# A hybrid decoder layer on one core: FFN buffers with a place of their own, and the last projection rows, norms and additions issued in other places

## The chip, the cores and the metric

The kernel runs on one core of a Trainium2 chip. The metric is the device time of one execution in microseconds (us). A core has a matrix engine (TensorE, PE in the profile, with its weight loads as PEld), a vector engine (VectorE, DVE), a scalar engine (ScalarE, ACT), a general engine (GpSimd, POOL) and a queue that issues transfers (SyncE, SP). Matrix products are written to PSUM, which has eight banks of 128 x 512 floats; everything else lies in SBUF, 128 partitions wide.

## The reference

One inference step of a one-layer decoder with D = 1024, for 16 meta rows, a prompt of 2048 rows and 8 x 4 sample rows. The rows that come out are 2048 + 32.

```
hp = layer_norm(concat(meta, x_prompt)); hs = layer_norm(x_sample)
mixed = token_mixers(h)            # one input projection, 4 retention heads, 4 gated DeltaNet heads,
                                   # gates, then  concat(o_r, o_g) @ w_out   (1024 x 1024)
h = layer_norm(ALPHA * h + mixed, ln1_g, ln1_b)
gu = h @ w_gate_up                 # 1024 x (2 * 2816)
f = (silu(gu[..., :2816]) * gu[..., 2816:]) @ w_down
y = layer_norm(ALPHA * h + f, ln2_g, ln2_b)
```

The states of both head groups and the last rows of the convolution are outputs too. All is float32. The change concerns only what stands after the token mixers: the output projection with its norm (ln1), the SwiGLU FFN, and its norm (ln2).

## The kernel before

Each float32 product is made of three fp32r products: both operands are split into a high part and a rest, and `mm3` (line 368) issues high x high, high x low and low x high into one PSUM accumulator. `split` makes the high part with a cast (line 311, on ScalarE) and the rest with a subtraction (line 318, on VectorE or GpSimd). The program is written with a framework that places buffers, orders the instructions of each engine by a simulated readiness with the program's order as priority, and adds all waits. A pool is a region of SBUF or PSUM; a tag with `bufs=n` has n slots. Pools are stacked: a pool that is opened after another one is closed takes its place, and then waits for the last use of what lay there. SP issues every transfer, in the order the framework gave it.

The kernel has three stages. `attention` (to about 1300 us) makes the mixed heads and stores them in device memory (`mixd`). `project` goes over 17 row tiles (16 of 128 rows, one of 32 sample rows) in the order of `BLOCKS`:

- `load(i)`: the mixed values into a staging tile `mr` (own tag, two slots), the residual rows into `oy`, and the split into `mh` and `ml`.
- `project(i)`: two halves of 512 columns, 24 matmuls each, in PSUM tag `d` (three banks, pool p_d); line 1199 adds the residual; `layer_norm` (ScalarE line 302, VectorE line 304 for the gain, GpSimd line 306 for the bias); the rows go to `yd`.
- `transposed(i)`: eight 128 x 128 transposes (line 1209) into PSUM tag `tr` (three banks, pool p_t), copies to `xr`. When both tiles of a pair are there, `sums` makes four differences on GpSimd (line 1222) and stores seven parts into `bd`: these are the seven token operands of a Strassen-Winograd scheme.

Its loop runs `project(i)`, the load of the next tile, and `transposed(i - 2)`; the last two iterations only transpose. The weights of the projection are four pieces, each loaded in two halves through the tag `raw` (two slots) and split into `wh`, `wl`.

`ffn` goes over three blocks of three row pairs. Block 0 has the prompt tiles P0 to P3 and the sample rows (n = 272 columns: two pairs of 128 and one of 16), blocks 1 and 2 six prompt tiles each (n = 384). `tokens(bi)` loads the seven token operands through the tag `fr` (four slots) and splits them into one tile each (pool f_b, ScalarE and VectorE). Then, for each of the 22 feature tiles f:

- `weights(f)` loads 1 MB of gate and up weights through `fr`, makes four sums and differences `S` on GpSimd (line 1288) and splits them; it is a generator that `step` advances.
- `gateup` issues seven products of 12 matmuls, into the PSUM tags X (two banks), Y, Z and W (pool p_g), with additions between them (line 1325), and applies the gate (lines 1331 to 1333). The result is `fh`, `fl`, in two halves: half 0 holds the first row tile of each pair, half 1 the second.
- `down` multiplies two feature tiles at a time with w_down (`dh`, `dl`): for every row tile and half of columns it issues 6 matmuls (3 for the last two feature tiles, which go one by one) into a `d` bank and adds the result to the row buffer `y` (line 1380). It is a generator too; `step`, called after each product of a later feature tile, takes one piece of it. In the last feature tile of all it takes three pieces.
- With the last pair of feature tiles of a block, each row tile's norm follows its additions: `layer_norm` with two statistics (line 286), their combination (line 289), eleven steps on one column (lines 263 to 270 and 299), then lines 302, 304 and 306. In the very last row tile lines 293 and 295 take the place of these three. The rows are then stored (line 1383).

The row buffers `y` are loaded (line 1429) after feature tile 1 of each block. The FFN's pools are opened after the projection's pools and its weights are closed, so they lie over them.

## Time and profile before

| | |
|---|---|
| median of 3 runs | 3042.78 us (3040.59 to 3043.56) |
| the profiled execution | 3041.72 us, span of its instructions 3039.9 us |
| granted TensorE clock, mean | 0.977 |
| TensorE busy | 2865.1 us (94%) |
| VectorE busy | 2184.7 us (72%) |
| ScalarE busy | 1148.7 us (38%) |
| GpSimd busy | 1039.0 us (34%) |
| memory traffic | 384.75 MB, mean 127 GB/s |

A line of a timeline has the start and the duration in us, the engine, the line of the kernel, the operation, and what it writes and reads. A line of the chain of work has start, duration, engine, tile and line; "issue" is time in which an engine waited for nothing that the profile shows. A line of a stage table has the stage, its length, and for PE, PEld, DVE, ACT and POOL the busy time with the number of instructions, then the granted clock, the share of the transfer engines and GB/s. A line of a tile's view has the operation, the number of records, the least, median and greatest duration in ns, the first and last start, and the shapes.

### The profile page before, as it was taken

To read this page: it belongs to the slowest core of one execution; us is meant where nothing else is said; L and a number is where in the kernel's file an instruction comes from. 1 tells how busy PE (TensorE), PEld (TensorE's weight loads), DVE (VectorE), ACT (ScalarE), POOL (GpSimd) and SP (SyncE) were. 2 spreads that over 40 slices of the span, in tenths; PEclk is the share of its full clock that TensorE was granted. 3 is DMA by queue.
4 is the path that set the end of the run, shared out by engine and by line. 5 is a ranking of instruction groups with operands and counts; after the bars stand their busy time and mean duration, and the time that the engine had idled before them with its cause. 6 is when DMAs were issued, how large, how long until landed. Compare 5 with 4: busy or idle time off the path is not lost.

```text
span 3039.9 us, 47059 instructions
## 1 busy us (share of the span) xinstructions
PE 2865.1 (94%) x17930; PEld 2550.1 (84%) x17930; DVE 2184.7 (72%) x4547; ACT 1148.7 (38%) x2571; POOL 1039.0 (34%) x927
## 2 busy tenths in 40 slices
PE   7999999999999999999869999899999989999995
PEld 6888888888888887978758889789999988999994
DVE  7777677766776676667677777886666688666667
ACT  2434444444444435432243333433333343233331
POOL 1222222221222131236545444453343335343332
PEclk9999999999999999999979999999999999999998
DMA  7544544443444333366542222431212244121211
GB/s 272 200 172 161 182 147 156 157 151 147 156 152 153 122 114 122 111 206 205 191 167 84 91 84 97 149 124 59 77 59 74 76 136 139 56 77 62 71 63 42
DMA packets 132274, 384.75 MB, mean 127 GB/s; under 512 B 18144, under 2 KB 53520, under 8 KB 115664
## 3 DMA queue, kind: packets, MB, share of 16 engines
q1 hardware_dynamic: 132048, 381.74, 36.0%
q8 instruction: 141, 2.31, 0.3%
q14 instruction: 85, 0.70, 0.1%
HBM read 294.14 MB, written 87.56 MB: 126 GB/s over the span
## 4 chain that ended last, share of the span: by engine, by line
PE 59%; DVE 21%; issue 6%; POOL 6%; ACT 4%; DMA 3%; SPq 0%; POOLq 0%; ACTq 0%; DVEq 0%
PE pj L368 18%; PE d L368 16%; PE Y L368 4%; PE X L368 4%; POOL S L1288 4%; PE Z L368 4%; PE W L368 3%; DVE dl L318 2%; DVE s34l L318 1%; ACT s34h L311 1%; DMA fr<-bd 1%; DVE cacc L822 1%; ACT junk L773 1%; DVE y L1380 1%; DVE lnst L286 1%
## 5 line engine op out<-in xcount | busy, mean ns | idle before, releaser
L368 PE MATMUL pj<-wh,xT 128*128 128x256 f32 (+2 forms) x2176 | 458.2, 294 | 8.4 <-ACT wh L311 4.2
L368 PE MATMUL pj<-xT,wh 128*128 128x512 f32 (+1 forms) x1280 | 379.8, 381 | 1.8 <-ACT cpre L806 1.1
L368 PEld LDWEIGHTS pj<-wh,xT 128*128 128x128 f32 (+1 forms) x2176 | 352.5, 187 | 13.1 <-ACT wh L311 4.4
L368 PE MATMUL pj<-wl,xT 128*128 128x256 f32 (+3 forms) x1088 | 309.8, 285 | 0.5 <-POOL wl L318 0.5
L368 PE MATMUL d<-dl,fh 128*128 128x512 f32 (+1 forms) x748 | 299.9, 401 | 9.2 <-DVE dl L318 8.6
L368 PE MATMUL d<-dh,fh 128*128 128x512 f32 (+1 forms) x748 | 294.0, 394 | 8.1 <-DVE y L1380 8.0
L368 PE MATMUL d<-dh,fl 128*128 128x512 f32 (+1 forms) x748 | 297.6, 398 | 2.1 <-POOL fl L318 2.1
L318 POOL TENSOR_TENSOR fl<-ta,fh 128x384 fp32r<-128x384 f32 (+1 forms) x66 | 70.9, 1074 | 642.7 <-ACT fh L311 642.7
L1288 POOL TENSOR_TENSOR S<-fr 128x512 f32<-128x512 f32 x132 | 209.8, 1607 | 168.9 <-DVE s34l L318 108.3
L1380 DVE TENSOR_TENSOR y<-y,d 128x512 f32<-128x512 f32 (+1 forms) x352 | 238.8, 680 | 31.4 <-PE d L368 31.2
L368 PEld LDWEIGHTS pj<-xT,wh 128*128 128x128 f32 x1280 | 211.9, 194 | 25.2 <-issue 3.4
L368 PE MATMUL pj<-xT,wl 128*128 128x512 f32 (+1 forms) x640 | 229.6, 359 | 0.0
L368 PEld LDWEIGHTS pj<-wl,xT 128*128 128x128 f32 (+1 forms) x1088 | 204.5, 188 | 0.9 <-POOL wl L318 0.8
L368 PEld LDWEIGHTS d<-dl,fh 128*128 128x128 f32 (+1 forms) x748 | 138.0, 184 | 40.3 <-DVE dl L318 22.3
L368 PEld LDWEIGHTS d<-dh,fl 128*128 128x128 f32 (+1 forms) x748 | 138.1, 185 | 35.5 <-POOL fl L318 2.6
L318 DVE TENSOR_TENSOR a11l<-fr,a11h 128x512 fp32r<-128x512 f32 x66 | 52.3, 792 | 158.1 <-ACT a11h L311 158.1
L368 PEld LDWEIGHTS d<-dh,fh 128*128 128x128 f32 (+1 forms) x748 | 137.9, 185 | 30.7 <-DVE y L1380 11.3
L311 ACT CAST a11h<-fr 128x512 fp32r<-128x512 f32 x66 | 41.0, 621 | 291.9 <-DMA fr<-gu 291.9
L368 PE MATMUL X<-b,a11h 128*128 128x384 f32 (+1 forms) x528 | 125.5, 322 | 18.1 <-ACT b L311 13.9
L822 DVE SCALAR_TENSOR_TENSOR cacc<-cpre,cw,cacc 128x512 f32<-128x512 f32 (+1 forms) x144 | 115.8, 805 | 32.0 <-ACT cacc L820 30.5
L368 PE MATMUL Y<-t,s34h 128*128 128x384 f32 (+1 forms) x528 | 128.8, 328 | 8.5 <-DVE u L1325 4.3
L368 PEld LDWEIGHTS pj<-xT,wl 128*128 128x128 f32 x640 | 122.7, 192 | 16.8 <-issue 0.8
(333 smaller groups left out, 7809.5 us busy)
## 6 DMA issues: line engine op xcount, KB each, us to landing
fr<-gu SPq DMA_DIRECT2D x132, 512.0 KB, 3.9
wh<-parts SPq DMA_DIRECT2D x45, 1024.0 KB, 5.0
wl<-parts SPq DMA_DIRECT2D x45, 1024.0 KB, 6.7
fr<-dn SPq DMA_DIRECT2D x66, 512.0 KB, 3.9
parts<-wh SPq DMA_DIRECT2D x15, 1024.0 KB, 5.3
parts<-wl SPq DMA_DIRECT2D x15, 1024.0 KB, 6.9
raw<-wret SPq DMA_DIRECT2D x16, 512.0 KB, 5.2
raw<-wgd SPq DMA_DIRECT2D x16, 512.0 KB, 7.1
```

The costliest lines, as they stand in the source:

```text
L286: i = nc.vector.bn_stats(out=st[:, o], in_=x)
L311: i = nc.scalar.copy(out=h, in_=src)
L318: i = (nc.vector if el == "dve" else nc.gpsimd).tensor_tensor(out=l, in0=src, in1=h.bitcast(F32), op=ALU.subtract)
L368: self.nc.tensor.matmul(out, lhsT=a(k), rhs=b(k), start=first and k == 0 and i == 0, stop=last and k == kn - 1 and i == 2, skip_group_chec ...
L773: nc.scalar.activation(out=junk, in_=p[:, j, :], func=AF.Square, accum_out=sq[:, a, t:t + 1])
L822: nc.vector.scalar_tensor_tensor(out=ac, in0=pre[:, i:i + N], scalar=w(i), in1=ac, op0=ALU.mult, op1=ALU.add)
L1288: op = lambda o, x, z, f: nc.gpsimd.tensor_tensor(out=o, in0=x, in1=z, op=f)
L1380: nc.vector.tensor_tensor(out=ys, in0=ys, in1=p, op=ALU.add)
```

## The change

- The order of the blocks: block 0 is now P0 to P5, block 1 P6 to P11, block 2 P12 to P15 and the sample rows (n = 272). The projection follows this order, so the sample rows come last.
- The FFN's pools f_r (loads), f_a (split weights), f_s (sums), f_b1 (the first two token operands, b11 and t2) and f_y (row buffers) are opened at the other end of SBUF, before the projection, and no longer over its buffers. So are the two PSUM pools. The projection's accumulators and its transposes both use the three `d` banks. `mr` is gone: the mixed values are staged in `raw`, which the output weights use too. `xr`, the differences `T` and the last two projected rows lie in the row buffers of f_y.
- The transposes of the last two projected tiles become a generator, `rest`, whose pieces are issued between the products of the FFN's first feature tile.
- The norms between blocks: `layer_norms` takes all row tiles of a group (the first tiles of the pairs, or the others) and makes the small steps once, on up to three columns. It is a generator as well and is issued piece by piece (`chores`) between later products. Each row tile's store is followed by the load of the next block's row buffer.
- The second piece of each token operand is subtracted on GpSimd, in blocks 1 and 2.
- The last feature tile of all: the products are in another order (`late`), the additions of the first row tiles come before the last product, and the split is on VectorE. `finish` then makes the other three row tiles: six accumulators in six banks, to each of which the row buffer is added by a matmul with the identity, in float32. `layer_norms` reads the sums from PSUM.

```diff
-    Block([(_P(0), _P(1), 128), (_P(2), _P(3), 128), (0, NS // 2, NS // 2)]),
-    Block([(_P(i), _P(i + 1), 128) for i in (4, 6, 8)]),
-    Block([(_P(i), _P(i + 1), 128) for i in (10, 12, 14)]),
+    Block([(_P(i), _P(i + 1), 128) for i in (0, 2, 4)]),
+    Block([(_P(i), _P(i + 1), 128) for i in (6, 8, 10)]),
+    Block([(_P(12), _P(13), 128), (_P(14), _P(15), 128), (0, NS // 2, NS // 2)]),
...
+    def layer_norms(self, work, g, b, pool, sums=None):
...
+        for i, (x, rows) in enumerate(work):
+            st = pool.tile([128, 2, 6], F32, tag="lnst", name="lnst")[:rows]
+            for o in range(2):
+                nc.vector.bn_stats(out=st[:, o], in_=sums[i][o] if sums else x[:, 512 * o:512 * o + 512])
+            nc.vector.bn_aggr(out=mv[:rows, i], in_=st)
+            yield
+        r = self.rsqrt(mv[:, :, 1], T, 128, pool, 1.0, LN_EPS)
...
+            if sums and i == T - 1:
...
+            for o, p in zip(at, src) if sums else [(slice(0, D), x)]:
+                nc.scalar.activation(out=x[:, o], in_=p, func=AF.Identity, scale=r[:rows, i:i + 1], bias=nm[:rows, i:i + 1])
+            nc.vector.tensor_tensor(out=x, in0=x, in1=g[:rows], op=ALU.mult)
+            for u, o in enumerate(at):
+                (nc.vector if sums and u else nc.gpsimd).tensor_tensor(out=x[:, o], in0=x[:, o], in1=b[:rows, o], op=ALU.add)
...
+        spare = lambda i: self.fy.tile([128, D], F32, tag=f"y{i}", name="spare")
...
-                raw = op.tile([128, 8, 128], F32, tag="mr", name="mr")[:, :, :rows]
+                raw = self.raw.tile([128, 4, 256], F32, tag="raw", name="raw").rearrange("p a b -> p (a b)").rearrange("p (a b) -> p a b", a=8)[:, :, :rows]
...
-            for i in range(N + 2):
-                if i < N:
-                    project(i)
-                    if i and i + 1 < N:
-                        load(i + 1)
+            for i in range(N):
+                project(i)
+                if i and i + 1 < N:
+                    load(i + 1)
                 if i >= 2:
-                    transposed(i - 2)
+                    for _ in transposed(i - 2):
+                        pass
+        return rest()
...
+                    product(Z, "s1", "t1")
+                    add(z5, u3, Z)
+                    add(u2, u2, Z)
+                    step(5)
+                    late(fh, fl)
+                    X = ps("X")
+                    product(X, "s4", "b22")
+                    add(u2, u2, X)
+                    swish(u2, z5, 1, "tb")
...
+            def finish(bi, fs, w, fi):
...
+                banks = [(pd, "d")] * 3 + [(pg, t) for t in "YWZ"]
...
+                        down1(blk, fs, w, fi, i, n, p, False)
+                        nc.tensor.matmul(p, lhsT=self.ident[:rows, :rows], rhs=y[i][:rows, 512 * n:512 * n + 512], start=False, stop=True)
...
-                        self.split(r, h[:, o:o + m], l[:, o:o + m], "act", "dve")
+                        self.split(r, h[:, o:o + m], l[:, o:o + m], "act", "pool" if u and bi else "dve")
...
-            units = []
+            units, chores = [rest], []
...
-                        if (bi, f) == end:
-                            per = 3
-                        else:
-                            per = 1 if f % 2 or i >= 2 else 0
-                        for _ in range(per):
-                            while units and next(units[0], self) is self:
-                                units.pop(0)
+                        for _ in range(3 if (bi, f) == end else 1 if f % 2 or i >= 2 or (bi, f) == (0, 0) else 0):
+                            some(units)
+                        for _ in range(2 if f == 2 else 1):
+                            some(chores)
                         next(ws, None)
...
-            with self.weights_es:
-                self.attention()
-                self.project()
-            self.ffn()
+            with ExitStack() as late:
+                with self.weights_es:
+                    self.attention()
+                    self.fr = self.pool("f_r", bufs=4, es=late, side="right")
+                    self.fa = self.pool("f_a", es=late, side="right")
+                    self.fs = self.pool("f_s", es=late, side="right")
+                    self.fb = self.pool("f_b1", es=late, side="right")
+                    self.fy = self.pool("f_y", es=late, side="right")
+                    self.pg = self.pool("p_g", space=PSUM, es=late)
+                    self.pd = self.pool("p_d", bufs=3, space=PSUM, es=late)
+                    rest = self.project()
+                self.ffn(rest)
```

231 lines of the change are left out of this document (150 added, 81 removed).

## The prediction

> **What bounds the kernel now.** I read the page first (busy shares, then the 40 slices), then one table of stages, then inside each bad stage the chain of work and the timeline. The page first:
>
> ```profile
> span 3039.9 us, 47059 instructions
> PE 2865.1 (94%) x17930; PEld 2550.1 (84%) x17930; DVE 2184.7 (72%) x4547; ACT 1148.7 (38%) x2571; POOL 1039.0 (34%) x927
> ...
> PE   7999999999999999999869999899999989999995
> ```
>
> TensorE is busy 94% of the span, so nothing that keeps the products as they are can gain more than some 175 us. The dips in the slices are the start, slice 19-20, slices 25 and 32, and the last one. The stage table (us, then busy time of PE, PEld, DVE, ACT, POOL, granted clock, DMA share, GB/s) puts sizes to them:
>
> ```profile
> 1290.00:1325.00 35.00, 30.68 (x172) 24.88 (x171) 20.87 (x55) 15.82 (x35) 7.12 (x3) 1.00 0.76 242
> 1325.00:1505.00 180.00, 180.00 (x851) 145.95 (x850) 128.77 (x259) 47.15 (x58) 103.62 (x74) 1.00 0.62 195
> 1505.00:1590.00 85.00, 47.99 (x279) 42.36 (x278) 61.23 (x75) 34.44 (x59) 44.94 (x32) 0.76 0.50 174
> 1930.00:2010.00 80.00, 65.21 (x320) 56.91 (x319) 78.22 (x139) 36.91 (x55) 38.60 (x27) 0.96 0.51 168
> 2460.00:2545.00 85.00, 72.58 (x332) 64.58 (x331) 83.51 (x157) 34.49 (x50) 41.95 (x27) 0.90 0.45 154
> 2996.00:3039.90 43.90, 11.37 (x40) 6.72 (x38) 37.59 (x108) 7.24 (x7) 13.86 (x11) 0.68 0.18 72
> 1540.00:1550.00 10.00, 9.11 (x50) 8.39 (x51) 6.49 (x12) 5.56 (x11) 0.00 (x0) 0.79 0.69 208
> ```
>
> TensorE idles 37.0 us at the passage from the output projection to the FFN (85 - 47.99), 14.8 and 12.4 us at the two passages between FFN blocks, 32.5 us in the tail, and 4.3 us where the projection starts. Inside the projection it never idles. Busy time at a lower clock is lost too: 9.11 us at 0.79 is 1.9 us, and the first passage has more of it before 1540. I count that passage as 41 us, the block passages as 16 each (their clocks 0.96 and 0.90), 110 us in all with the tail and the start. The change touches every one of these places and, outside them, only the projection.
>
> **First passage (project to ffn), term +30.** The chain of work there, in order of time:
>
> ```profile
> 1494.86 10.94 PE d L368 x48
> ...
> 1515.54 1.27 POOL oy L306
> ...
> 1523.79 2.03 DMA bd<-T
> 1525.88 4.07 DMA fr<-gu
> ...
> 1534.93 1.60 POOL S L1288
> ...
> 1540.07 1.50 PE X L368 x5
> ```
>
> The last projection matmul ends at 1505.8 (1494.86 + 10.94); then follow the last norm (to 1516.8), the last transposes and differences, their stores, and only then (1525.88) the first weight load, because the FFN buffers lie over the projection's. The change gives f_r, f_a, f_s, the first two token tiles and f_y their own place, so that the loads, casts and S sums of feature tile 0 and the tiles b11 and t2 need nothing of the projection's end (block 0 becomes P0 to P5, whose parts are stored in the first half of the projection). The last two tiles' transposes are issued between the first products instead. What is late next are the other five token tiles: f_b lies over the projection's weights, so their casts can start only when its last matmul is done.
>
> ```profile
> L311 ACT CAST b<-fr x5: 617/622/1055, 1926.8 to 1951.7; 128x512 fp32r<-128x512 f32 x3, 128x1024 fp32r<-128x1024 f32 x2
> L318 DVE TENSOR_TENSOR b<-fr,b x5: 686/693/1218, 1927.5 to 1953.1; 128x512 fp32r<-128x512 f32 x3, 128x1024 fp32r<-128x1024 f32 x2
> fr<-bd SPq DMA_DIRECT2D x14, 512.0 KB, 3.6
> ```
>
> A 1536-column tile costs ACT 1.05 + 0.62 = 1.7 us, VectorE 1.22 + 0.69 = 1.9 us, and 768 KB of load. Four fr buffers can hold t1 and b21 before the end, so from the last projection matmul t1 is ready at about +3.2 and b21 at +5.5; t3, t4 and b22 wait for a free buffer, 3.6 us of landing and 1.9 us of VectorE, which I put at +9.5, +12.5 and +15.5. A product at n = 384 is 12 matmuls of 384 columns: with 48 matmuls of 512 in 10.94 us, 0.228 each, an estimate of 0.17 each, 2.0 us. Seven take 14 us, the transposes 1.8, so feature tile 0 ends near +17.5, 2 us late. Feature tile 1's weights queue behind the tokens on SP (land near +16.5), then two S sums of 1.60 and a split: about 4 us late. The last norm's VectorE work, earlier in the program, competes: 5 us. That leaves 11 of 41. Ends: 5 left (+36) if the last is hidden; 21 left (+20) if none of the loads really moves ahead of the projection's end.
>
> **Block passages, +10 and +6.** VectorE is 98% busy in both (78.22 of 80, 83.51 of 85), so it is the bound. What fills it:
>
> ```profile
> 1930.00:2010.00 80.00, 9.44 (x15) 0.96 0.51 168
> 1930.00:2010.00 80.00, 10.95 (x15) 0.96 0.51 168
> 1930.00:2010.00 80.00, 2.60 (x5) 0.96 0.51 168
> 1930.00:2010.00 80.00, 0.70 (x5) 0.96 0.51 168
> ```
>
> These are lines L269, L270, L299 and L264: the one-column steps of five layer norms. With four kinds of 0.14 us (L263 to L267) a norm's 11 small steps cost 1.89 + 2.19 + 0.52 + 0.56 = 5.2 us, 0.47 us each. layer_norms does up to three rows' statistics at once: 13 steps for a group, two groups, 26 steps instead of 55, so 13.6 us less. The second piece of each token tile goes to POOL: 7 x 0.69 = 4.8 us less on VectorE. That is 18 us less than 78, below the 65 us of products, so VectorE stops being the bound. Next late are the token loads (four buffers, tiles replaced one by one as the last feature tile frees them) and the gate weights behind them on SP. The rows also go through SP in a new order, each y load right behind its out store; a wait there holds the next gu load queued behind it. I leave 6 us of 16 at the first and 10 at the second passage, where the last block has 272 columns (1.5 us a product) over the same queue. Ends for both together: +5 and +26.
>
> The split moved to POOL has its own price. The trace has the same one-column step beside a POOL operation and without one (start, duration, engine):
>
> ```profile
> 1461.96 2.52 POOL L1222 TENSOR_TENSOR T<-xr 128x512 f32<-128x512 f32 x2
> 1462.05 1.21 DVE L270 SCALAR_TENSOR_TENSOR rqy<-rqt,rqy 128x1 f32<-128x1 f32 x1
> ...
> 1467.14 0.16 DVE L270 SCALAR_TENSOR_TENSOR rqy<-rqt,rqy 128x1 f32<-128x1 f32 x1
> ```
>
> So a VectorE step can stretch to the POOL operation's 1.2 us. The splits above have medians of 0.69 in a stage where POOL is half busy, so I take no extra charge. The Trainium skill ("SBUF — State Buffer", the term "shared port pair") says that VectorE and GpSimd arbitrate for one port pair, held for a whole instruction, and that the loser fully blocks; the 1.21 against 0.16 agrees. By that rule seven POOL splits of 1.2 us could stop VectorE for 8 us a block, more than the 4.8 saved, and the sum below would be about 38 instead of 42.
>
> **Tail, +7.** Now the tail is VectorE's: TensorE waits for the additions, and the norms run one by one.
>
> ```profile
> PE d L368 <- DVE y L1380: 6.5, 4, 3.0
> 2996.14 0.56 DVE L1325 TENSOR_TENSOR u<-u,Z 128x384 f32<-128x384 f32 x1 [1.24 <-PE Z L368]
> 2999.68 1.01 POOL L318 TENSOR_TENSOR fl<-tb,fh 128x384 fp32r<-128x384 f32 x1 [4.95 <-ACT fh L311]
> 3012.91 0.63 PE L368 MATMUL d<-dl,fh 128*128 128x512 f32 x1
> 3033.43 2.92 POOL L306 TENSOR_TENSOR y<-y,b 128x512 f32<-128x512 f32 x2 [3.11 <-DVE y L304]
> L674 PE MATMUL pj<-ub,rkd x16: 587/587/692, 71.3 to 363.6; 32*128 32x512 f32 x16
> ```
>
> After it, from the end A of the last gate/up product: sum, tanh and split take 4.55 us now (2996.14 to 3000.69); with 272 columns about 3.5, and 1 more for the first group's norm on VectorE. Then six groups, each three matmuls of 0.228 and the identity addition. That one is full fp32: the nearest row has 16 records for 8 such matmuls of 512 columns at 587 ns, against about 390 for fp32r that start every 228, so about 2 x 0.42 = 0.85. Six times 1.53 is 9.2. TensorE idled 4.5 us before; the matmul at 3012.91 takes 0.63 instead of 0.39 after a wait of 3.0, so the first of them run slow: +2. Then the last statistics and 13 small steps without POOL, 3.5; two rows of (1.21 + 0.67) and four half-row steps of 0.74, 6.7; store and end as now, 3039.9 less the last POOL addition's end at 3036.35, 3.5. Together 29.4, of which 4.1 is work that must run anyway: 25.3 lost against 32.5. Ends: 2 (the small steps stretch) and 15 (the first group's norm hidden, no slow clock).
>
> **What the change costs, -7 and -4.** The staging tile mr shares the raw ring (two buffers) with the four output weights. The rows of now:
>
> ```profile
> 1286.67 1.58 SPq L340 DMA_DIRECT2D raw<-wout  x2
> 1296.62 1.00 SPq L1183 DMA_DIRECT2D mr<-mixd  x2
> 1301.46 1.04 ACT L311 CAST mh<-mr 128x1024 fp32r<-128x1024 f32 x1
> 1302.59 4.73 POOL L318 TENSOR_TENSOR ml<-mr,mh 128x1024 fp32r<-128x1024 f32 x2 [17.02 <-ACT mh L311]
> 1316.16 24.44 PE d L368 x107
> ```
>
> Today weights and two rows of mixed values load side by side. Afterwards mr of tile 0 holds one raw buffer until its subtraction ends near 1305, half of the second weight comes after that, and mr of tile 1 comes last of ten loads. At 4.5 us a load and 2 us a split I get tile 1 ready at 1325.5 and two tiles done by 1336.4 (48 matmuls later); now the 107 matmuls that end at 1340.6 close the third tile, so two are done at 1329.7: -6.7, taken as -7, ends -2 (the order is better than I trace it) and -11.
>
> The projection's transposes now share the three "d" banks. An accumulator must be evacuated while the eight transposes run:
>
> ```profile
> 1470.41 0.87 PE tr L1209 x8
> 1469.96 0.68 DVE L1199 SCALAR_TENSOR_TENSOR oy<-oy,d 128x512 f32<-128x512 f32 x1
> 1471.28 0.67 DVE L1199 SCALAR_TENSOR_TENSOR oy<-oy,d 128x512 f32<-128x512 f32 x1
> ```
>
> Here it would be free at 1471.95, 0.67 after the transposes; at prompt tiles it is free in time. Fifteen tiles at 0 to 0.9 us (the transposes' own 0.87 at most, by this row): I take -4, ends 0 and -13. Weights and two token tiles add some 8 us to VectorE's 128.77 of 180, hidden there. Splitting feature half 1 on VectorE and the reordering of the blocks cost nothing elsewhere: the product count is the same.
>
> **Sum.** 30 + 10 + 6 + 7 - 7 - 4 = 42 us. The profiled execution took 3041.72 us, 1.06 below the median of 3042.78, so the forecast is 3001. All ends together give 3 to 75 us.
>
> **Rivals.** (1) The loads do not really run ahead: the scheduler keeps them behind the projection on SP's queue or behind late buffers. Then the first passage gains 20, the blocks 8, the tail 4, and the costs stay at 11: 21 us, 3022. For it: the order on SP decides, and it is not visible. Against: wout and mr loads did run ahead of the attention's end. (2) All passages close: VectorE relieved, tokens ahead: 36 + 24 + 12 - 5 = 67, 2976. Against it are the token loads with four buffers. (3) Slower: the projection, the one stage at 180.00 of 180, stalls at every tile because three banks wait for VectorE, which is 72% busy and now has splits of 1.2 us in its queue. The gains without that term are 46, so from 2.7 us at each of 17 tiles it decides; at 4 us it costs 68 and the kernel takes about 3064. Against it: the wait seen is 0.7. (4) No change, gains eaten by the start and the banks: 3042.
>
> **How the numbers follow.** Forecast 57% (its own range 2985 to 3012), rival 1 20%, rival 2 12%, rival 3 7%, no change 4%. The range 2974 to 3027 leaves out part of rivals 1 and 2, and all of rival 3 and of no change. Differences under 0.2% (6 us) this measurement can't tell from none. Forecast, rivals 1 and 2 are faster, together 0.89; same 0.04; slower 0.07.
>
> **What would show it.** Right: first weight and b11 loads long before the projection's last matmul; TensorE idle under 15 us in the first passage, clock near 1; VectorE below 90% at the block passages with 26 small steps; the tail from the last gate/up product near 30 us; TensorE idle 8 us or more at the start of the projection. Wrong: gu loads still after the last projection matmul, a wait for the evictions (L1199) or copies before every product of the projection, or VectorE as full as now at the block passages.

## The result and the profile after: 15 us slower, not 42 faster

The changed kernel takes 3058.10 us in the median of four runs (3057.22 to 3059.72); the ratio to the kernel before is 1.0054, 95% interval 1.0036 to 1.0071. The forecast was 3001. The profiled execution has a span of 3055.7 us against 3039.9. The head of its page, and its slices:

```profile
span 3055.7 us, 46987 instructions
PE 2887.7 (95%) x17942; PEld 2563.1 (84%) x17942; DVE 2157.1 (71%) x4423; ACT 1147.9 (38%) x2572; POOL 1065.7 (35%) x937
...
PE   7999999999999999989989999998999999889997
```

Counted from 0 as in the prediction, the dips at slices 19 and 20 and in the last slice are smaller than before. A new one is at slice 17, where the projection starts, and the two at the block passages are now at 27 and at 34 and 35. The stage table of the changed kernel (columns as in the prediction):

```profile
1290.00:1318.00 28.00, 17.08 (x116) 14.30 (x114) 16.78 (x50) 13.15 (x33) 2.36 (x1) 0.81 0.62 205
1318.00:1534.80 216.80, 208.52 (x938) 166.88 (x939) 149.19 (x287) 58.60 (x71) 118.31 (x80) 0.97 0.58 185
1534.80:1595.00 60.20, 45.40 (x232) 42.29 (x231) 43.64 (x55) 26.71 (x44) 30.72 (x23) 0.88 0.69 224
2045.00:2180.00 135.00, 118.04 (x579) 105.98 (x578) 113.21 (x159) 53.03 (x77) 75.76 (x48) 0.95 0.43 147
2590.00:2705.00 115.00, 90.27 (x487) 77.40 (x487) 90.52 (x146) 44.82 (x75) 71.15 (x48) 0.85 0.40 133
3022.20:3055.70 33.50, 14.12 (x54) 8.03 (x52) 25.90 (x62) 6.10 (x9) 9.47 (x6) 0.79 0.17 67
```

The six rows are the end of attention, the projection, the first passage, the two block passages and the tail. In what follows, the loss of a stage is TensorE's idle time plus its busy time times the missing share of the clock, summed over stretches of 5 us; read from the rows above it comes out within 2 us of that (the second block passage: 115 - 90.27 = 24.7 idle, 90.27 x 0.15 = 13.5). Where a stretch is taken to end moves a loss by up to 1 us.

| stage (us) | before | after | change | forecast |
|---|---|---|---|---|
| last product of attention's projection | at 1296.3 | at 1298.7 | +2.4 | 0 |
| from there to the last output-projection product | 208.6 | 234.4 | +25.8 | +11 |
| loss of the first passage | 43.8 | about 20 | -24 | -30 |
| loss of the two block passages | 17.5 and 20.0 | 21.6 and 36.5 | +21 | -16 |
| tail: idle, plus 5.1 us of added identity products | 32.5 | 19.4 + 5.1 | -8 | -7 |
| sum | | | +17 | -42 |

The measured difference of the spans is +15.8. The first row is no effect of the change: in the runs below attention's last product starts anywhere from 1293 to 1304. Two of the gains came, that of the first passage smaller than forecast and that of the tail about as forecast. Two places went wrong: the projection costs 26 instead of 11, and the block passages lost 21 where 16 were to be won. The experiments take these places one by one.

### The profile page after: what moved, and what is told of

It is laid out like the page before. It is cut to its first block, busy times and chain, and to the rows that moved or that the text cites. A ratio compares the mean times of both kernels' runs of the same rounds, so it can differ in the third digit from the quotient of the medians.

```text
span 3055.7 us, 46987 instructions
## 1 busy us (share of the span) xinstructions
PE 2887.7 (95%) x17942; PEld 2563.1 (84%) x17942; DVE 2157.1 (71%) x4423; ACT 1147.9 (38%) x2572; POOL 1065.7 (35%) x937
## 4 chain that ended last, share of the span: by engine, by line
PE 64%; DVE 20%; ACT 4%; DMA 4%; POOL 4%; issue 3%; SPq 0%; ACTq 0%; POOLq 0%; DVEq 0%
PE pj L405 18%; PE d L405 16%; PE X L405 5%; PE Y L405 5%; PE Z L405 5%; PE W L405 3%; DVE dl L355 3%; POOL S L1328 2%; DMA fr<-bd 1%; DVE s34l L355 1%; ACT s34h L348 1%; DMA fr<-gu 1%; ACT junk L810 1%; DVE cacc L859 1%; DVE tb L1374 1%
## 5 line engine op out<-in xcount | busy, mean ns | idle before, releaser
L355 DVE TENSOR_TENSOR dl<-fr,dh 128x1024 fp32r<-128x1024 f32 x66 | 130.8, 2008 | 4.8 <-ACT dh L348 4.7
L960 POOL TENSOR_TENSOR Lm<-LT,lvl 128x512 f16<-128x512 f32 (+1 forms) x108 | 129.3, 1230 | 11.3 <-DVE LT L948 10.5
```

The costliest lines, as they stand in the source:

```text
L355: i = (nc.vector if el == "dve" else nc.gpsimd).tensor_tensor(out=l, in0=src, in1=h.bitcast(F32), op=ALU.subtract)
L960: nc.gpsimd.tensor_tensor(out=Lm[:, x - 1], in0=LT, in1=lvl(x), op=ALU.mult)
```

## The experiments

All times are medians; ratios are to the kernel before, measured beside each run, with their 95% intervals. Stages are read from one profiled execution of each kernel. Each diff is against the changed kernel, on top of the kernel that the text names. The theory for the projection was a cost of space (PSUM banks and staging buffers that wait for their last user), its rival one of order in the engines' queues. For the block passages one theory was GpSimd's queue, the other the transfers on SP.

### The projection: a place in PSUM, the staging, the banks

**psum_order**: of the two PSUM pools, p_d (the accumulators) is opened ahead of p_g.

```diff
+                    self.pd = self.pool("p_d", bufs=3, space=PSUM, es=late)
                     self.pg = self.pool("p_g", space=PSUM, es=late)
-                    self.pd = self.pool("p_d", bufs=3, space=PSUM, es=late)
```

> The changed kernel with the two PSUM pools opened in the other order, so that the three accumulator banks of the projection lie over the first banks of the attention instead of its last ones. Theory A (place in PSUM): the projection's first product waits in the changed kernel for the attention's last copy out of PSUM (it starts at 1318.0, against 1303.4 before); with other banks it starts near 1304 and the kernel is 10 to 15 us faster than the changed one, about 3045. Rival B (staging in the raw ring): the order of loads is the real limit at the start, the first product moves up but the second half of the weights and row tile 1 do not, three row tiles are done no earlier than 1350 (1355 in the changed kernel), and the time falls by less than 5 us.

3053.99 us, 1.0040 (1.0021 to 1.0059). The projection's first products read `mh`; the row of the tile gives their first and last start. The kernel before, the changed kernel, and psum_order:

```profile
L368 PE MATMUL d<-wh,mh x272: 389/389/504, 1303.4 to 1504.9; 128*128 128x512 f32 x128, 128*32 128x512 f32 x8
```

```profile
L405 PE MATMUL d<-wh,mh x272: 387/389/795, 1318.0 to 1533.1; 128*128 128x512 f32 x128, 128*32 128x512 f32 x8
```

```profile
L405 PE MATMUL d<-wh,mh x272: 387/389/792, 1304.3 to 1529.2; 128*128 128x512 f32 x128, 128*32 128x512 f32 x8
```

One line moved the first product from 1318.0 to 1304.3. With p_g opened first, p_d came to lie over the banks that attention uses last, and the first product had to wait for their last reader. TensorE's waits in the changed kernel from 1290 to 1535 (for whom, us in total, times, longest) show both that wait (line 694, the last mixed values) and the one that I come to below (line 1272, the residual addition):

```profile
PE d L405 <- DVE oy L1272: 5.7, 6, 1.9
...
PE d L405 <- ACT mx L694: 1.7, 1, 1.7
```

The wait itself reads only 1.7 us, because TensorE had stood at attention's last steps until just before (10.9 us idle from 1290 to 1318); in psum_order projection products fill that time, and their start is 14 us earlier. Of these the stage got 6.7 back (234.4 to 227.7): the staging is late next.

**tr_own_banks**: the transposes of all but the last two tiles get two banks of their own, tag X of p_g, which stands unused until the FFN.

```diff
-                p = self.pd.tile([128, 512], F32, tag="d", name="tr")...
+                p = (self.pg.tile([128, 512], F32, tag="X", name="tr", bufs=2) if i < N - 2 else self.pd.tile([128, 512], F32, tag="d", name="tr"))...
```

> The changed kernel with the transposes of the projection in the two X banks, which stand empty there, so that the accumulators have the three d banks for themselves. Theory A (shared banks): the projection's 13.6 us of stalls between its first and last product, against before, come from evictions that must end before the next product; they go and the kernel is 8 to 14 us faster, 3045 to 3050. Rival C (queue order): the stalls come from token casts and subtractions of the first FFN block that stand ahead of the evictions in the queues of ScalarE and VectorE and wait there for a load; then the banks only let TensorE run one accumulator further, and less than 5 us come back.

3046.15 us, 1.0011 (1.0002 to 1.0021). The same row:

```profile
L405 PE MATMUL d<-wh,mh x272: 387/389/794, 1318.5 to 1517.5; 128*128 128x512 f32 x128, 128*32 128x512 f32 x8
```

From first to last it is 199.0 us, against 215.1 with shared banks and 201.5 before. The sharing cost 16 us, and no wait for line 1272 is left in this stage. (In the changed kernel's row of this stage 8.3 us are idle time, 216.80 - 208.52, and some 6 the granted clock of 0.97.) What made an evacuation late is seen in the chain of work of the changed kernel (start, duration, what), at two places:

```profile
1352.80 1.23 DVE oy L306
1354.02 0.61 DVE oy L1272
...
1354.77 0.64 PE tr L1216 x4
...
1385.16 4.91 DMA bd<-spare
...
1390.13 4.11 DMA fr<-bd
...
1394.26 1.06 ACT b L348
...
1395.34 1.23 DVE b L355
1396.57 0.61 DVE oy L1272
...
1397.22 2.79 PE d L405 x11
```

At 1354 the addition that frees a bank stood in VectorE's queue behind the gain multiplication of the row tile before (line 306). At 1396 it stood behind the split of an early token operand, which waited for its load, which waited for the store of the differences. With banks of their own for the transposes the same queues cost nothing in this stage: what was missing was banks.

**mixed_staging**: the mixed values staged in two row buffers of f_y that are still free.

```diff
-                raw = self.raw.tile([128, 4, 256], F32, tag="raw", ...)...
+                raw = (spare(4 + i % 2) if i < N - 2 else self.raw.tile(...))...
```

> The changed kernel with the mixed values staged in two row buffers of the FFN (y4 and y5, unused there until the last two row tiles), not in the raw ring. Rival B (staging decides the start): 5 to 8 us faster, row tile 1 ready ten us earlier. Theory A (place in PSUM): the first product still waits until 1318 for its bank, the loads are done by then more fully, and 2 to 6 us come back at most, because the weights' second half arrives while the first products run.

3061.70 us, 1.0068 (1.0048 to 1.0088): slower than the changed kernel. The first product started at 1328.7, after TensorE had waited 8.9 us for `mh`. Those row buffers lie over a region that attention frees late: SP issued the first load at 1323.14, when the store of attention's last mixed values had landed. It says nothing against the staging as a cost; it put a second wait in its place.

**projection_repaired**: psum_order, tr_own_banks and mixed_staging together.

> All three edits together: accumulator banks over the attention's first banks, transposes in the X banks, mixed values staged in row buffers. If the three causes add up (start 14.6 and the staging behind it, stalls 13.6), 22 to 30 us come back: 3028 to 3036, faster than the kernel before. If token instructions in the queues cause the stalls (C), about 15 to 20 come back: 3038 to 3043.

3053.39 us, 1.0038 (1.0023 to 1.0053); the stage took 227.0 us, with the first product at 1318.5 and a wait of 8.5 us for `mh`. The place of the staging spoiled what the other two gave.

**order_and_banks**: psum_order and tr_own_banks, the staging as in the change.

> The changed kernel with the transposes of the projection in the X banks, and the PSUM pools opened in the other order. The first alone took the stalls between the projection's first and last product away (216 to 199 us) and left the late start (1318.5). Theory A (place in PSUM): with the other order the first product starts near 1304 and, nothing else holding it, the projection ends 10 to 14 us earlier than with the X banks alone (1518), a span near 3032. Rival B (staging): the products start at 1304 but wait for the second half of the weights, loaded through the same ring as the mixed values, and the projection ends less than 6 us earlier, a span of 3039 or more.

3039.26 us, 0.9985 (0.9975 to 0.9995); the stage 213.2 us, the first product at 1305.6. What is left is the ring of two buffers, seen in this kernel's chain of work:

```profile
1308.80 4.18 DMA raw<-wout
...
1315.34 4.60 DMA raw<-wout
...
1322.30 4.44 DMA raw<-mixd
...
1327.89 2.38 POOL ml L355
...
1330.31 14.80 PE d L405 x64
```

Two halves of a weight and a mixed tile come one after another, each behind the split that frees its buffer.

**own_staging**: order_and_banks with the staging tile on its own tag of two, as before the change, paid for with one of the two early token operands.

```diff
-                raw = self.raw.tile([128, 4, 256], F32, tag="raw", ...)...
+                raw = op.tile([128, 8, 128], F32, tag="mr", name="mr")[:, :, :rows]
...
-                    t = (self.fb if j < 2 else bp).tile(...)
+                    t = (self.fb if j < 1 else bp).tile(...)
```

> X banks and pool order as in order_and_banks, and the mixed values staged in a tag of their own again (two tiles, as before); the room for it comes from loading only one token tile (b11) ahead, not two. Staging theory (B, what is left of the late start): from the attention's last projection product to the output projection's last one it is 208.6 us before, 234.4 changed, 213.2 in order_and_banks; with the weights and mixed values in separate rings it falls to 206 to 209. The first passage then loses 0 to 5 us more than its 20, because t2 is loaded late. Rival: the ring makes no difference, 212 or more, and the rest comes from loads of the FFN that run at the same time.

3036.20 us, 0.9983 (0.9971 to 0.9996). The stage took 207.8 us, the 208.6 of the kernel before: the projection's 26 us are all accounted for, 16 by the banks and 10 by the start. Of the start, the place in PSUM alone is 5 (218.4 to 213.2) and the staging 5 (213.2 to 207.8). The median fell by only 3 of these last 5, which its uncertainty allows. That this run also loads one token operand less ahead does not explain it: with none ahead, in no_early_tokens below, the stage takes 218.8 us against 218.4.

### The first passage: what do the early token operands bring?

**no_early_tokens**: tr_own_banks with all token operands in f_b, none ahead of the projection's end.

```diff
-                    self.fb = self.pool("f_b1", es=late, side="right")
...
-                    t = (self.fb if j < 2 else bp).tile([128, 2, 4 * 384], F32R, ...)
+                    t = bp.tile([128, 2, 4 * 384], F32R, ...)
```

> X banks, and no token tile loaded ahead of the projection's end (b11 and t2 lie with the other five over its weights); weights and S sums of feature tile 0 still come early. The prediction's chain makes the early tiles worth their casts and subtractions, 3.6 us, at least: the first passage loses 23 to 27 us instead of 19, and the projection does not change (218 from the attention's last projection product to its own). Rival: token loads ahead of the end also hold ScalarE's and VectorE's queues in the projection, and without them the projection gets 3 us or more shorter, with no change in all.

3045.42 us, 1.0006 (0.9997 to 1.0015), against 3046.15; the passage lost 18.6 us against 19.2. The two early operands are worth nothing that shows. What holds this passage is on two queues. TensorE's longest wait there, in the changed kernel, is for the norm of the last row tile, whose bias is added on GpSimd:

```profile
PE tr L1216 <- POOL spare L308: 9.0, 1, 9.0
```

And SP, in the same kernel (start, duration, line, transfer):

```profile
1553.83 0.95 SPq L1314 DMA_DIRECT2D fr<-gu  x2
1554.83 17.85 SPq L1237 DMA_DIRECT2D bd<-spare  x10
```

The weights of feature tile 1 were issued at 1553.83, 20 us after the last projection product, and those of tile 2 stood 17.85 us behind ten stores of differences, the last of which waited for GpSimd: it made these differences at 1569.89, behind four sums `S`.

### The block passages: relieved VectorE, and slower

**tokens_on_vector**: tr_own_banks with the second piece of each token operand on VectorE again.

```diff
-                        self.split(r, h[:, o:o + m], l[:, o:o + m], "act", "pool" if u and bi else "dve")
+                        self.split(r, h[:, o:o + m], l[:, o:o + m], "act", "dve")
```

> Transposes in the X banks, and all subtractions of the token tiles on VectorE as in the kernel before. Against the X banks alone (TensorE's lost time, idle and slow clock, 23 us at the first block passage and 37 at the second). Theory D (GpSimd became the bound): the seven pieces stand in GpSimd's queue before the S sums and the low halves of f; without them the two passages lose 10 us or more less, 50 or below together. Rival: VectorE was the bound and takes them back at 0.7 us each; the passages lose as much as now or up to 10 more.

3038.28 us, 0.9983 (0.9973 to 0.9993), 7.9 less than tr_own_banks; the passages lost 20.1 and 35.8 us against 23.3 and 36.7, so 4 of the 8 are in them; where the rest is, is not shown.

**norms_as_before**: tr_own_banks with a norm for each row at the passages, and the row buffers loaded after feature tile 1.

```diff
-                            if last and n and i == group[-1]:
+                            if last and n and bi < end[0]:
+                                self.layer_norm(y[i][:rows], rows, g2, b2, sm)
+                                nc.sync.dma_start(out=self.O["y"][...], in_=y[i][:rows])
+                            elif last and n and i == group[-1]:
                                 chores.append(normed(bi, group))
...
-                    if (bi, f) == (0, 1):
+                    if f == 1:
```

> Transposes in the X banks, and at the two block passages the norms row by row inside the last additions and the loads of the row buffers after feature tile 1, as in the kernel before; the last group norm and the tail stay as changed. Theory E (the grouped norm's bias additions stand in one row in GpSimd's queue, and the row loads hold SP's queue): the passages lose 12 us or more less than the 60 of the X banks alone. Rival (the prediction's): the one-column steps, 55 instead of 26, fill VectorE again, 14 us more of it at each passage, and the passages lose as much as now or more.

3041.73 us, 0.9994 (0.9983 to 1.0004), 4.4 less than tr_own_banks; the passages lost 25.0 and 27.4 us against 23.3 and 36.7. The grouped norm, made to relieve the passages, costs 9 us at the second one together with its new place for the row loads (the edit undoes both), and gains 2 at the first. The two intervals overlap a little.

**blocks_as_before**: tr_own_banks with the old order of blocks (272 columns first). The sixth row buffer is then loaded at the first block passage.

```diff
-    Block([(_P(i), _P(i + 1), 128) for i in (0, 2, 4)]),
-    Block([(_P(i), _P(i + 1), 128) for i in (6, 8, 10)]),
-    Block([(_P(12), _P(13), 128), (_P(14), _P(15), 128), (0, NS // 2, NS // 2)]),
+    Block([(_P(0), _P(1), 128), (_P(2), _P(3), 128), (0, NS // 2, NS // 2)]),
+    Block([(_P(i), _P(i + 1), 128) for i in (4, 6, 8)]),
+    Block([(_P(i), _P(i + 1), 128) for i in (10, 12, 14)]),
```

> Transposes in the X banks, and the order of the blocks as in the kernel before: the block with the sample rows (272 columns) first, two blocks of 384 columns after it. Theory F (cover): a passage into a block of 272 columns has 10.6 us of products for each feature tile instead of 14 and the same chores; with 384 columns after both passages they lose 20 us or less each, 40 instead of 60 together, while the first passage, now into 272 columns, loses 3 to 8 more than its 19: a gain of 10 to 15. Rival: the columns do not matter, the second passage loses 30 or more as now.

3035.78 us, 0.9974 (0.9961 to 0.9987), 10.4 less than tr_own_banks. The second passage lost 21.7 us instead of 36.7; the first passage (projection to FFN) 24.1 instead of 19.2, the tail 24.9 instead of 20.6. So the small block at the end gains 9 at those two ends and loses 15 at the block passage into it.

**short_token_loads**: tr_own_banks with only 32 columns of each token operand of blocks 1 and 2 loaded, and spread over the tile.

> X banks, and in blocks 1 and 2 each token load brings only its first 32 columns (16 KB in place of up to 512); casts and subtractions read these 32 again and again, so all other work keeps its size. It leaves out most of the token data of blocks 1 and 2. Theory G (landing of the token loads bounds the passages): the 60 us lost at both with the X banks alone fall to 40 or less. Rival H (the engines' queues and GpSimd's share of them): 52 or more stay.

3036.02 us, 0.9977 (0.9968 to 0.9987). The passages lost 16.6 and 34.0 us, 50.6 against 60.0: between the theories. Transfers are part of the first block passage's loss, little of the second's.

**no_bias_passages**: tokens_on_vector without the bias additions of the grouped norm at the passages and of the last block's first group. The result lacks these biases.

```diff
-            for u, o in enumerate(at):
+            for u, o in enumerate(at) if sums else []:
                 (nc.vector if sums and u else nc.gpsimd).tensor_tensor(out=x[:, o], in0=x[:, o], in1=b[:rows, o], op=ALU.add)
```

> The kernel tokens_on_vector with one thing left out: the bias additions of the grouped norm at both passages and of the last block's first group (GpSimd, 1.5 to 1.8 us each, four in a row in the second passage), so the result lacks that bias. Theory 1 (the second passage is held by GpSimd's queue, the four bias additions standing ahead of the low halves and the S sums): the two passages lose 20.1 + 35.8 us in tokens_on_vector and lose about 18 + 28 here, and the median is 8 to 11 us under that kernel's. Rival (the row loads behind the out stores on SP hold it, and GpSimd only waits with them): the passages keep their loss within 2 us each, and the median moves by less than 4 us.

3016.63 us, 0.9913 (0.9895 to 0.9932): 21.7 us less than tokens_on_vector, twice what theory 1 expected. The passages lost 9.6 and 22.7 us instead of 20.1 and 35.8. The stage rows of tokens_on_vector, then of no_bias_passages:

```profile
2040.00:2165.00 125.00, 110.44 (x533) 98.22 (x532) 109.49 (x157) 48.39 (x73) 64.06 (x41) 0.95 0.43 148
2570.00:2685.00 115.00, 90.93 (x494) 77.59 (x493) 96.89 (x150) 43.51 (x75) 63.51 (x46) 0.85 0.42 139
```

```profile
2040.00:2165.00 125.00, 116.41 (x592) 105.85 (x591) 108.00 (x169) 55.06 (x81) 46.03 (x31) 0.99 0.46 157
2565.00:2670.00 105.00, 89.12 (x510) 76.84 (x509) 93.82 (x153) 45.69 (x78) 48.04 (x33) 0.92 0.47 154
```

With the additions GpSimd is busy 51% and 55% of the two stages (64.06 of 125, 63.51 of 115), and yet its work costs the passages that much. The kernel before has nearly as many of these additions there (10 and 12, now 12 and 12), so the 21.7 us are what they cost in all, not what the change added. Before, they come in pairs, one row tile at a time; now up to four row halves follow one another. GpSimd's timeline in the second passage (start, duration, line, operation), before and changed:

```profile
2506.17 2.53 POOL L306 TENSOR_TENSOR y<-y,b 128x512 f32<-128x512 f32 x2 [2.63 <-DVE y L304]
2515.71 2.54 POOL L306 TENSOR_TENSOR y<-y,b 128x512 f32<-128x512 f32 x2 [7.01 <-DVE y L304]
```

```profile
2640.39 7.27 POOL L342 TENSOR_TENSOR y<-y,b 128x512 f32<-128x512 f32 x4 [1.64 <-DVE y L340]
2647.63 2.86 POOL L355 TENSOR_TENSOR fl<-tb,fh 128x256 fp32r<-128x256 f32 x2
...
2679.86 6.83 POOL L342 TENSOR_TENSOR y<-y,b 128x512 f32<-128x512 f32 x4
2686.65 1.56 POOL L355 TENSOR_TENSOR fl<-tb,fh 128x256 fp32r<-128x256 f32 x2
```

Four bias additions in a row take 7 us, and the low half `fl` that the down products need stands behind them. SP waits as well, in the same kernel, and the row loads (line 1450) and the next gate weights stand behind its stores:

```profile
2678.70 8.35 SPq L1442 DMA_DIRECT2D out_y<-y  x3
2687.14 1.20 SPq L1450 DMA_DIRECT2D y<-yd  x2
2688.44 0.44 SPq L1314 DMA_DIRECT2D fr<-gu  x1
```

In no_bias_passages the same three stores take 2.24 us of SP:

```profile
2644.41 2.24 SPq L1442 DMA_DIRECT2D out_y<-y  x3
```

TensorE's longest wait in this passage, 6.4 us, goes that way. The chain of work follows it from the four additions at 2679.86 through the stores to the row loads, and on to TensorE:

```profile
2687.14 4.33 DMA y<-yd
...
2691.60 0.70 DVE y L1464
...
2692.34 6.45 PE d L405 x18
```

The wait for this row addition (line 1464) is 6.6 us in tr_own_banks and 0.8 in norms_as_before, which loads the rows later; without the bias additions it is 3.3, against 8.2 in tokens_on_vector. No wait of TensorE in the changed kernel's second passage ends with `fl`.

There is a third way, in neither theory. VectorE and GpSimd hold each other up, as the changed kernel's timeline shows at the first block passage:

```profile
2058.34 2.36 DVE L355 TENSOR_TENSOR dl<-fr,dh 128x1024 fp32r<-128x1024 f32 x2 [0.16 <-ACT dh L348]
...
2118.77 1.57 POOL L342 TENSOR_TENSOR y<-y,b 128x512 f32<-128x512 f32 x1
2119.14 2.28 DVE L355 TENSOR_TENSOR s34l<-S,s34h 128x1024 fp32r<-128x1024 f32 x1
...
2121.34 4.22 DVE L355 TENSOR_TENSOR dl<-fr,dh 128x1024 fp32r<-128x1024 f32 x2
...
2123.41 0.79 PE L405 MATMUL d<-dl,fh 128*128 128x512 f32 x1 [6.11 <-DVE dl L355]
```

At 2058 GpSimd is idle when the two subtractions `dl` start, and they take 2.36 us together. At 2119 a bias addition is running when `s34l` starts, which then takes 2.28 instead of 1.2, and the two `dl` behind it, beside GpSimd's next work, take 4.22. GpSimd's two sums `S` that run beside these `dl` take 4.47 us; the next one, at 2126.66, takes 1.28. TensorE's longest wait of this block passage, 6.1 us, ends with the `dl`.

**short_row_stores**: tr_own_banks with only 32 columns of each normed row stored.

```diff
-                    nc.sync.dma_start(out=self.O["y"][tiles[j][0]:sum(tiles[j]), :], in_=y[j][:tiles[j][1]])
+                    nc.sync.dma_start(out=self.O["y"][tiles[j][0]:sum(tiles[j]), :32], in_=y[j][:tiles[j][1], :32])
```

> The kernel tr_own_banks with the stores of the normed rows cut to their first 32 columns, so most of the output is left out; the row loads that wait for these stores get their buffers at once. Rival (the row loads behind the out stores hold the second passage): its loss of 36.7 us falls to 28 or less, the median by 7 us or more. Theory 1 (GpSimd's queue of bias additions): the second passage keeps 34 to 38 us, the first its 23, and the median falls by less than 4 us.

3046.69 us, 1.0011 (1.0002 to 1.0021), no different from tr_own_banks; the passages lost 24.2 and 36.1 us. SP stands as long at the stores as with whole rows:

```profile
2664.44 7.87 SPq L1442 DMA_DIRECT2D out_y<-y  x3
```

So the stores' length is not what SP waits for, and the rival falls in the form in which it was tested. That the row loads stand behind the stores is not refuted by this run, since the stores still wait for the bias additions (19.9 us in six waits around the second passage). Three ways lead from the bias additions to TensorE: GpSimd's own queue (`S`, `fl`), SP's (`y`, gate weights), and VectorE's instructions that run longer beside them. How the 22 us divide among the three these runs don't tell.

### The tail

**tail_add_on_vector**: tr_own_banks with the last row buffers added on VectorE, as before the change, and not by the identity.

```diff
-                        down1(blk, fs, w, fi, i, n, p, False)
-                        nc.tensor.matmul(p, lhsT=self.ident[:rows, :rows], rhs=y[i][...], start=False, stop=True)
+                        down1(blk, fs, w, fi, i, n, p)
+                        nc.vector.tensor_tensor(out=p, in0=p, in1=y[i][...], op=ALU.add)
```

> X banks, and the last three row tiles' residual added on VectorE into the row buffer, as in the kernel before, and not by identity matmuls; statistics read the row buffer. By the prediction's terms TensorE needs 1.53 us for each of six groups with the addition and VectorE 1.36 without: the tail (from the last gate/up product to the end) changes by less than 2 us. Rival: the additions on TensorE are what shortened the tail, and it gets 4 us or more longer.

3048.42 us, 1.0019 (1.0010 to 1.0029), against 1.0011 (1.0002 to 1.0021): the intervals overlap. The tail lost 28.2 us against 20.6 and 5.1 of identity products, so the identity is worth about 2.5, between what the theory and its rival expected. Its price in the changed kernel's chain of work:

```profile
3030.80 0.86 PE d L1485 x2
```

### What the parts give together

**combined**: order_and_banks, tokens_on_vector and blocks_as_before.

> X banks, pool order, token subtractions on VectorE and the old block order together. If the effects add (against X banks alone: -5 for the pool order, -3 to -4 for the tokens, -9 for the blocks), the span is near 3027 and the kernel 0.4 to 0.6% faster than the one before. If the attention's end and the staging eat the pool order's part, 3031.

3026.98 us, 0.9951 (0.9936 to 0.9966).

**best_kernel**: combined with no_early_tokens and, in the space that this frees, the staging on its own tag of two.

> X banks, pool order, old block order, token subtractions on VectorE, no token tile ahead (worth nothing in no_early_tokens), and in the room of these the mixed values staged on their own. Against combined (span 3024, median 3027): the attention's last to the projection's last product falls from 213 to 207 or 208, the rest stays: 3020 to 3024. If the first passage needs the early tiles once the block before it is short, 3026.

3020.86 us, 0.9930 (0.9915 to 0.9945). The projection took 208.0 us; the block passages lost 23.6 and 17.0, the first passage 22.1, the tail 24.7.

**best_row_norms**: best_kernel with norms_as_before.

> best_kernel with the norms at the block passages row by row and the row buffers loaded after feature tile 1, as before. If the grouped norm gives anything (the prediction's 14 us less on VectorE at each passage), this kernel is 8 us or more slower than best_kernel. If the passages are bound by something else, it is within 5 us of it.

3020.77 us, 0.9929 (0.9914 to 0.9944): no difference. In the restored block order the grouped norm neither costs nor gains, so the 9 us above belong to the grouped norm and the new block order together.

**best_half_bias**: best_kernel with the second half of each bias addition on VectorE.

```diff
-                (nc.vector if sums and u else nc.gpsimd).tensor_tensor(out=x[:, o], in0=x[:, o], in1=b[:rows, o], op=ALU.add)
+                (nc.vector if u else nc.gpsimd).tensor_tensor(out=x[:, o], in0=x[:, o], in1=b[:rows, o], op=ALU.add)
```

> best_kernel with the second 512 columns of every bias addition at the passages on VectorE instead of GpSimd (as the tail already has it); the whole computation is done. Theory 1 (GpSimd's row of bias additions delays the out stores, the row loads behind them and the first additions of the next block, also in best_kernel's block order, where the two passages lose 23.6 and 17.0 us): five additions of about 1.7 us fewer on GpSimd per passage against 0.67 us each more on VectorE; the passages lose 3 to 6 us less together and the median is 3014 to 3018. Rival (once the block order is restored the bias is hidden, and VectorE is what the passages wait for): 6.7 us more work on VectorE over both passages, the median is 3021 to 3026.

3015.69 us, 0.9913 (0.9897 to 0.9930): the fastest that does the whole computation; the kernel before took 3041.54 in the same series. The intervals of this kernel and best_kernel overlap a little; the stages say where the 5 us are. The passages lost 18.3 and 13.0 us instead of 23.6 and 17.0. That is 9 us and not 5, because the profiled execution of best_half_bias, at 3010.88, is the fastest of its four. Its first passage has more work on VectorE (third busy column). best_kernel, then best_half_bias:

```profile
1910.00:2010.00 100.00, 81.86 (x395) 72.12 (x394) 87.66 (x130) 40.75 (x61) 51.93 (x36) 0.91 0.46 158
```

```profile
1905.00:2005.00 100.00, 85.62 (x415) 75.55 (x415) 92.38 (x139) 43.07 (x66) 46.84 (x31) 0.95 0.48 165
```

With VectorE busy 92.38 us of 100 instead of 87.66, TensorE is busy 85.62 instead of 81.86. The passage with the fuller VectorE and less work on GpSimd is the faster one.

## Why the prediction was wrong

- **Block passages, +10 and +6: the failed step, measured -21.** The premise was "VectorE is 98% busy in both ..., so it is the bound". The relief came: the step on one column that took 9.44 us in 15 instructions takes 0.9 and 1.5 in 6, and VectorE is 84% and 79% busy (113.21 of 135, 90.52 of 115). The passages lost 58 us instead of 37.5 all the same. So VectorE's amount of work was not what they waited for: best_kernel and best_row_norms, with the grouped norm and without, take the same time. What the runs showed in its place is the bias additions on GpSimd, which the prediction did not price at all because they stayed there; leaving them out gives back 21.7 us. Of what the change did at these places, undoing the block order gives back 10.4, the token splits 7.9, the norms with their row loads 4.4. The words "a wait there holds the next gu load queued behind it" named one of the ways, SP's, and the prediction still took 10 and 6 us of gain. The 272-column block was taken as a matter of 1.5 us a product; its price, 15 us at that passage, was not seen. By which way the additions cost most stays open.
- **Shared banks, -4: mis-sized, measured -16**, beyond its end of -13. The prediction took the additions' delay from tiles that are prompt (0.67 us). In this stage an addition also stands behind a gain multiplication of 1.23 us or a token split that waits for its load, and both rows above end in a wait of TensorE. Rival 3 had part of this mechanism ("splits of 1.2 us in its queue"), but at 16 us over 17 tiles it is 1 us a tile, not the 2.7 from which it would have decided alone.
- **Start, -7: measured -10.** The staging was seen, and is 5 of it. Not seen was where the PSUM pools come to lie. The diff moves both pools, and the step said nothing of what their banks held before; that is the other 5 us.
- **First passage, +30: mechanism right, measured +24.** 20 us stayed instead of 11. The loads did move ahead: the first split of `S` starts at 1341.1 (the `s12l` row at the end of this text), 190 us before the projection's end. Two terms were too small. The last norm was taken as 5 us: the transposes of the last row tile, issued between the first products, waited 9.0 us for it, and the slower clock behind that wait took 3 more. The weights of feature tile 1 were to land at +16.5 and were issued at +20, and the differences' stores, which the sum did not have on SP, held those of tile 2 for 17.85 us. The early token operands, on which the sum leaned, are worth nothing.
- **Tail, +7: measured +8, in part by luck.** The identity products took the 0.85 us each that the prediction had. But the stretch from the last gate and up product to the end took 33.5 us instead of 29.4, and it came out right because the products that had to run in it took 9.0 us (14.12 less 5.1) instead of 4.1. To TensorE's restart it took 7.4 us (3022.2 to 3029.6) instead of 4.5, and from the last bias addition to the end 6.5 instead of 3.5. The slow products, priced at 2, cost 0.3 (the first four 0.30 us each instead of 0.23).
- **The port pair.** The tokens' split on GpSimd cost 3 to 4 us in the passages and 8 in the median, by tokens_on_vector, where the prediction took a gain of 4.8 on VectorE and no charge. By the rule that the prediction quoted from the Trainium skill ("SBUF — State Buffer", the term "shared port pair") the splits would have cost more than they saved, and the trace agrees with that sign; how much of it is the port and how much GpSimd's queue no run here separates.

## What to carry to other kernels

An engine that is 98% busy in a stage need not be what the stage waits for, and part of that share can be time in which another engine holds it up. Before relieving it, follow what the next stage's first products need through every queue, the half-idle ones too, and ask what now stands ahead of it there. When pools move, write down for each bank and buffer what used it last; a relocated accumulator can hold a whole stage's start for a wait that reads 1.7 us. And buffers given up to make room are paid where the queue that empties them is late, not where it is prompt.

## What was not expected of the hardware

- A bias addition of 512 columns on GpSimd has no fixed price: four take 7.27 us at 2640.39 (1.8 each), one 1.26 at 2677.41, in the chain of work of the same passage.
- The granted clock is low where TensorE has waited: 0.85 over the 115 us of the second passage in the changed kernel, and 0.99 in the first block passage without the bias additions (0.95 with them). Of the 36.5 us lost in that second passage, 11.8 are slow clock and not idle time.
- VectorE's subtraction `dl` takes 2.3 us in the median where `s12l` of the same shape takes 1.2, in both kernels. It is the hold-up shown at the block passages, all through the FFN: of the changed kernel's 66 `dl`, 49 take over 1.5 us, and each of these starts while a GpSimd instruction is running; of the 15 that start with GpSimd free, none takes that long. The busy share of VectorE contains this time. The rows (least, median, greatest in ns, first and last start):

```profile
L355 DVE TENSOR_TENSOR s12l<-S,s12h x66: 1211/1226/2289, 1341.1 to 2990.4; 128x1024 fp32r<-128x1024 f32 x66
...
L355 DVE TENSOR_TENSOR dl<-fr,dh x66: 1205/2307/2317, 1592.8 to 3011.3; 128x1024 fp32r<-128x1024 f32 x66
```
